# The last token block's norm, divided between GpSimd and VectorE, with its second half in one PSUM bank

## The chip, the cores and the metric

The kernel runs on one core of a Trainium2 chip. The metric is the time of one execution on the device in microseconds. A core has five engines with instruction streams of their own: TensorE (PE in the profile; its weight loads are PEld), VectorE (DVE), ScalarE (ACT), GpSimd (POOL) and SyncE (SP). They work on SBUF, TensorE writes its products into PSUM, which is divided into banks of 512 f32 columns by 128 partitions, and DMA queues move data between SBUF and HBM.

## The reference

Two transformer layers over 512 tokens of width 1024, in float32. Layer 0 mixes with latent attention, layer 1 with sliding-window attention; each layer then has an MLP of inner width 4096. After every part comes a layer norm of the scaled input plus the part's output:

```python
def _layernorm(x, g, b):
    xf = x.astype(jnp.float32)
    mu = xf.mean(-1, keepdims=True)
    var = jnp.square(xf - mu).mean(-1, keepdims=True)
    return ((xf - mu) * lax.rsqrt(var + LN_EPS) * g + b).astype(x.dtype)

def _mlp(x, w_up, w_down):
    h = jax.nn.relu(x @ w_up)
    return (h * h) @ w_down

def reference(...):
    ...
    for l in range(DEPTH):
        ...
        x = _layernorm(alpha * x + y, ln_mix_g[l], ln_mix_b[l])
        x = _layernorm(alpha * x + _mlp(x, mlp_w_up[l], mlp_w_down[l]), ln_mlp_g[l], ln_mlp_b[l])
    return x
```

The change concerns the very last of these norms, that of layer 1's MLP, whose result is the output.

## The kernel before

Products in float32 are made of three matmuls each: both factors are split into a high and a low part (`split`), and `three` lists high by high, high by low and low by high. The 512 tokens are four blocks of 128 (`NT` = 4). The last stage of each MLP is a `TokMajor` product: tokens lie on the partitions, the 1024 output columns are two halves of 512, and the sum over 1024 inner features runs over four weight chunks `kp` of two feature blocks each, so a block of tokens by half of the columns takes 24 matmuls.

`TokMajor.finish` first runs the first half of the columns, chunk by chunk over the four token blocks (`part`, which hands a block's bank to `evac` after its last chunk). It then fetches all four weight chunks of the second half, and goes through the token blocks one by one: 24 matmuls into a bank, `evac`, and the block's `layer_norm`. For the last norm (`dst is None`) of the last block, the second half is two accumulations of 256 columns, each into a bank of its own.

Here `evac` is `add_last`: VectorE adds the bank to the token rows `xs[t]` in SBUF (`add_plain`, L563) and `count` gathers the statistics (`bn_stats`, L553; in pieces of 256 columns for the last block, of 512 for the others). `layer_norm` aggregates them (L419), lets GpSimd raise the variance to the power -1/2 (`rsqrt_of`, L398), and makes two passes on VectorE: subtract the mean and multiply by the gain (L422), multiply by the rsqrt and add the bias (L425). The last block's second pass is cut at 512 and 768, and SyncE stores each cut (L428); the other blocks are stored whole.

PSUM tiles come from a ring of six full banks (`bank`), whatever their width; a bank comes free when the last user of its tile is done. The order of the instructions on an engine is set by a planner that reckons the time of each and issues what is ready by priority: earlier program order first, and what stands in `tc.high_priority()` ahead of the rest. Only what is passed to `pe` (all matmuls here) keeps the program's order; `pin` does so for VectorE in other stages, and not in this one. The planner also puts in the semaphores between engines that use the same tile.

Of the kernel before, what the change touches and what calls it, by code (L numbers as in the profile page):

```python
# [8 lines left out]
F32 = mybir.dt.float32  # L9
F32R = mybir.dt.float32r  # L10
AF = mybir.ActivationFunctionType
ALU = mybir.AluOpType
# [3 lines left out]
P = 128  # L16
D = 1024
S = 512
NT = S // P
# [29 lines left out]
def build(tc, nc, io, out):  # L49
    with ExitStack() as top:  # L50
# [3 lines left out]
        sp = top.enter_context(tc.tile_pool(name="sp", bufs=1))  # L54
# [7 lines left out]
        def nm(s):  # L62
            n_names[0] += 1
            return f"{s}_{n_names[0]}"

        def bank(cols=512, tag="mm", bufs=6):
            return ps.tile([P, cols], F32, tag=tag, bufs=bufs, name=nm(tag), padded_shape=[P, 512])
# [17 lines left out]
        def pe(ins):  # L85
            tc.keep_in_program_order(ins)

        pinned = [False]
# [8 lines left out]
        def pin(ins):  # L97

            if pinned[0]:
                pe(ins)  # L100

        def group(dst, pairs, first=True, last=True, **kw):
            for i, (st, mv) in enumerate(pairs):
                pe(nc.tensor.matmul(  # L104
                    dst, st, mv, start=first and i == 0, stop=last and i == len(pairs) - 1, **kw
                ))
# [186 lines left out]
        state = {"next": 0, "at": 0, "hold": 0}  # L293
# [6 lines left out]
        def prepare(n):  # L300

            state["hold"] += n
            while state["next"] < state["hold"]:
                prep(state["next"])
                state["next"] += 1

        def weights(name):
            i = state["at"]
            state["at"] += 1
            while state["next"] < len(stream):  # L310
                on_ring = len([j for j in range(i, state["next"] + 1) if not off_ring[j]])
                if on_ring > AHEAD or state["next"] >= state["hold"] or (off_ring[state["next"]] and mlp_pool[0] is None):
                    break
                prep(state["next"])
                state["next"] += 1
            got, wh, wl = ready.pop(i)
            assert got == name
            return wh, wl
# [7 lines left out]
        class Feat:  # L326


            def __init__(self):
                self.hs, self.ls = xt_pair()  # L330
# [13 lines left out]
        b = bank()  # L344
# [51 lines left out]
        def rsqrt_of(v):  # L396
            r = sp.tile([P, 1], F32, tag="rs", bufs=8, name=nm("rs"))
            nc.gpsimd.tensor_tensor(r, v, half, ALU.pow)  # L398
            return r


        xs = [None] * NT

        def load_gb(which, l):

            if which == "mix":
                gb = [mlp_pool[0].tile([P, D], F32, tag=tag, bufs=1, name=nm("gb")) for tag in ("a12", "a22")]
            else:
                both = gp.tile([P, 2, D], F32, tag="gb", bufs=1, name=nm("gb"))
                gb = [both[:, 0, :], both[:, 1, :]]  # L410
            for to, of in zip(gb, "gb"):
                pe(nc.sync.dma_start(to, io[f"ln_{which}_{of}"][l].partition_broadcast(P)))
            return gb

        def layer_norm(t, gb, dst):

            x = xs[t]
            mv = sp.tile([P, 2], F32, tag="mv", bufs=4, name=nm("mv"))
            pin(nc.vector.bn_aggr(mv, stats[t]))  # L419
            stats[t] = None  # L420
            r = rsqrt_of(mv[:, 1:2])
            pin(nc.vector.scalar_tensor_tensor(x, x, mv[:, 0:1], gb[0], ALU.subtract, ALU.mult))  # L422
            cuts = (0, 512, 768, D) if dst is None and t == NT - 1 else (0, D)
            for c in map(slice, cuts, cuts[1:]):
                state["norm"] = nc.vector.scalar_tensor_tensor(x[:, c], x[:, c], r, gb[1][:, c], ALU.mult, ALU.add)  # L425
                pin(state["norm"])
                if dst is None:
                    nc.sync.dma_start(out[t * P : (t + 1) * P, c], x[:, c])  # L428

        def turn_tokens(t, dst):  # L430

# [19 lines left out]
        class TokMajor:  # L451
# [4 lines left out]
            def __init__(self, src, evac, name):  # L456
                self.src, self.evac, self.name = src, evac, name
                self.w, self.b, self.done = [], {}, set()

            def group(self, b, t, kp, w, cols=slice(0, 512)):  # L460
                tk = slice(t * P, (t + 1) * P)
# [5 lines left out]
            def part(self, t, kp):  # L467
                while len(self.w) <= kp:
                    self.w.append(weights(self.name))
                if t not in self.b:  # L470
                    self.b[t] = bank()
                self.group(self.b[t], t, kp, self.w[kp])
                self.done.add((t, kp))
                if kp == 3:
                    self.evac(t, slice(0, 512), self.b[t])

            def finish(self, gb=None, dst=None, early=None):

                for kp in range(4):
                    for t in range(NT):
                        if (t, kp) not in self.done:
                            self.part(t, kp)
                if gb is not None:
                    ws = [weights(self.name) for _ in range(4)]
                    if callable(gb):
                        gb = gb()
                    for t in range(NT):
                        n = 2 if dst is None and t == NT - 1 else 1  # L490
                        for i in range(n):
                            c = slice(i * 512 // n, (i + 1) * 512 // n)
                            b = bank(512 // n)
                            for kp in range(4):
                                self.group(b, t, kp, ws[kp], c)
                            pinned[0] = early
                            with tc.high_priority():
                                self.evac(t, slice(512 + c.start, 512 + c.stop), b)
                            pinned[0] = False
                        pinned[0] = early  # L500
                        with tc.high_priority():
                            layer_norm(t, gb, dst)
                        if early:
                            prepare(early[t])
                        pinned[0] = False
                        if dst is not None and t in (1, 2):
                            with tc.high_priority():
                                dst.turn(t - 1)
                else:
                    bs = [bank() for _ in range(NT)]  # L510
                    for kp in range(4):
                        w = weights(self.name)
                        for t in range(NT):
                            self.group(bs[t], t, kp, w)
                    for t in range(NT):
                        self.evac(t, slice(512, D), bs[t])
# [27 lines left out]

        stats = [None] * NT

        def count(t, c):

            n = 256 if t == NT - 1 else 512
            if stats[t] is None:  # L550
                stats[t] = sp.tile([P, D // n, 6], F32, tag="bn", bufs=4, name=nm("bn"), padded_shape=[P, 4, 6])
            for i in range(c.start // n, c.stop // n):
                pin(nc.vector.bn_stats(stats[t][:, i, :], xs[t][:, i * n : (i + 1) * n]))  # L553
                if i == 0:

                    m2 = stats[t][:, 0, 2:3]
                    pin(nc.vector.tensor_scalar(m2, m2, LN_EPS * D, None, ALU.add))
# [7 lines left out]
        def add_scaled_last(t, c, b):  # L565
            add_scaled(t, c, b)
            count(t, c)

        def add_last(t, c, b):
            add_plain(t, c, b)  # L570
            count(t, c)
# [310 lines left out]
        with tc.tile_pool(name="mla", bufs=1) as mp:  # L882
# [108 lines left out]
            ws = [weights("w_q") for _ in range(4)]  # L991
# [98 lines left out]
            ws = [weights("w_qr"), weights("w_qr")]  # L1090
            qb = {}
            for t, rs in ((0, (0, 1)), (1, (0, 1)), (0, (2,)), (1, (2,)), (2, range(3)), (3, range(3))):
                tk = slice(t * P, (t + 1) * P)
                if 0 in rs:
                    qb[t] = bank()
                for r in rs:
                    wh, wl = ws[r // 2]
                    c = slice((r % 2) * 512, (r % 2 + 1) * 512)
# [110 lines left out]
        gb = lambda: load_gb("mix", 0)  # L1209
# [10 lines left out]
        with tc.tile_pool(name="swa", bufs=1) as mp:  # L1220
# [55 lines left out]
            def queries(m, part):  # L1276
                if part == 0:
                    qb[m] = (weights("w_sq"), bank())
                w, b = qb[m]
                feat_major(x2, w, b, ks=range(4 * part, 4 * part + 4))  # L1280
                if part == 1:
                    load_bias(m)
                    with tc.high_priority():
                        query_parts(m, slice(0, S), b)
# [118 lines left out]
        gb = lambda: load_gb("mix", 1)  # L1403
# [115 lines left out]
```

## Time and profile before

| what | value |
|---|---|
| median of 3 runs | 997.08 us (996.8 to 997.32) |
| span of the profiled execution | 997.4 us |
| TensorE busy in the span | 986.3 us (99%) |
| VectorE busy | 771.9 us (77%) |
| ScalarE busy | 554.7 us (56%) |
| GpSimd busy | 216.5 us (22%) |
| start of the last matmul | 989.76 us |
| start of the last store | 994.34 us |

The profiled execution has no time of its own beside its span; the three runs are timed apart from it. A row of a timeline is: start in us, length in us, engine, line, operation, output<-inputs, shapes, count, and in brackets the idle time before it with what ended it. A row of the groups is: line, engine, operation, tiles, shapes, count, then busy time in us and the mean in ns of one, then the idle time of the engine just before them. "SPq" and "ACTq" are the queues that issue DMAs. A row of the issues ends with the time in us from an issue to its landing. The ends of matmuls are modelled; their starts are measured.

### The profile page before, as it was taken

How to read it: one execution, taken by the hardware profiler on the slowest of the kernel's cores; microseconds unless marked ns; L12 is line 12 of the kernel's file. 1: busy time of each engine (PE TensorE's matmuls, PEld its weight loads, DVE VectorE, ACT ScalarE, POOL GpSimd, SP SyncE). 2: the span in 40 equal slices, each digit the busy share in tenths (PEclk: the TensorE clock that was granted, in tenths of full speed). 3: DMA queues.
4: the chain of work that ended last, by engine and by line, in shares of the span. 5: the costliest groups of instructions: out<-in, count | busy, mean ns of one | idle time of the engine just before them, and what ended most of it. 6: DMA issues, size and time to landing. Idle time of an engine off the chain costs nothing.

```text
span 997.4 us, 15835 instructions
## 1 busy us (share of the span) xinstructions
PE 986.3 (99%) x6107; PEld 890.0 (89%) x6107; DVE 771.9 (77%) x1243; ACT 554.7 (56%) x850; POOL 216.5 (22%) x203
## 2 busy tenths in 40 slices
PE   9999999999999999999999999999999999999997
PEld 8988888998999999998898998889998999999986
DVE  5589967989778769877586778698985986898756
ACT  5457643467537637636145888546763664664620
POOL 0231101122212211210002775212131122123000
PEclk9999999999999999999999999999999999999999
DMA  7431126389879977963232212259798798798422
GB/s 249 143 89 54 64 106 224 92 174 243 157 171 241 175 174 202 230 118 125 87 106 96 85 65 75 96 158 208 195 187 187 166 214 175 162 263 147 117 93 85
DMA packets 60679, 149.55 MB, mean 150 GB/s; under 512 B 5260, under 2 KB 10301, under 8 KB 60605
## 3 DMA queue, kind: packets, MB, share of 16 engines
q0 software_dynamic: 24320, 58.73, 32.9%
q1 hardware_dynamic: 36140, 89.56, 27.1%
q8 instruction: 48, 0.79, 0.3%
q10 hardware_dynamic: 144, 0.26, 0.1%
q14 instruction: 27, 0.21, 0.1%
HBM read 146.41 MB, written 4.22 MB: 151 GB/s over the span
## 4 chain that ended last, share of the span: by engine, by line
PE 96%; DVE 2%; ACT 1%; DMA 1%; issue 0%; POOL 0%; DVEq 0%; SPq 0%; ACTq 0%
PE mm L104 88%; PE tr L104 5%; PE tr L1159 1%; PE tr L663 1%; PE tr L1348 1%; ACT wh L77 1%; PE tr L1350 0%; DMA raw<-in_w_kv 0%; PE tr L437 0%; DMA raw<-in_w_h 0%; DVE mm L1320 0%; DVE ptl L80 0%; PE tr L924 0%; DVE ql L80 0%; POOL wl L80 0%
## 5 line engine op out<-in xcount | busy, mean ns | idle before, releaser
L104 PE MATMUL mm<-wh,fac 128*128 128x512 f32 (+1 forms) x944 | 292.8, 387 | 0.0
L77 ACT ACTIVATE wh<-wq 128x1024 fp32r<-128x1024 f32 x164 | 173.6, 1060 | 183.6 <-PE mm L104 131.4
L80 DVE TENSOR_TENSOR wl<-wq,wh 128x1024 fp32r<-128x1024 f32 x164 | 199.7, 1222 | 70.9 <-ACT wh L77 70.1
L104 PE MATMUL mm<-xth,wh 128*128 128x256 f32 (+1 forms) x928 | 243.7, 291 | 0.0
L104 PE MATMUL mm<-xth,wl 128*128 128x256 f32 (+1 forms) x800 | 233.5, 292 | 0.0
L104 PEld LDWEIGHTS mm<-wh,fac 128*128 128x128 f32 x944 | 176.3, 188 | 35.4 <-DVE fac L80 0.6
L104 PE MATMUL mm<-xtl,wh 128*128 128x256 f32 (+1 forms) x672 | 197.4, 294 | 0.0
L104 PE MATMUL mm<-wl,fac 128*128 128x512 f32 (+1 forms) x472 | 182.4, 387 | 0.0
L104 PEld LDWEIGHTS mm<-xth,wh 128*128 128x128 f32 x928 | 168.9, 192 | 3.1
L104 PEld LDWEIGHTS mm<-xth,wl 128*128 128x128 f32 x800 | 153.4, 192 | 2.6
L77 ACT ACTIVATE wh<-raw 128x1024 fp32r<-128x1024 f32 (+3 forms) x86 | 85.0, 989 | 95.1 <-PE mm L104 56.4
L199 POOL DMA_DIRECT2D wq<-in_up x64 | 77.5, 1228 | 257.7 <-DVE wl L80 189.0
L104 PEld LDWEIGHTS mm<-xtl,wh 128*128 128x128 f32 x672 | 128.9, 192 | 3.0
L80 DVE TENSOR_TENSOR wl<-raw,wh 128x1024 fp32r<-128x1024 f32 (+2 forms) x66 | 77.1, 1174 | 35.1 <-ACT wh L77 34.7
L104 PEld LDWEIGHTS mm<-wl,fac 128*128 128x128 f32 x472 | 88.9, 188 | 16.6
L199 POOL DMA_DIRECT2D wq<-in_down x48 | 42.0, 875 | 187.5 <-DVE wl L80 181.6
L80 POOL TENSOR_TENSOR wl<-raw,wh 128x1024 fp32r<-128x1024 f32 (+2 forms) x20 | 41.2, 2063 | 87.6 <-ACT wh L77 81.9
L104 PE MATMUL mm<-wh,oh 128*128 128x512 f32 x128 | 50.9, 398 | 0.0
L104 PE MATMUL mm<-wh,ol 128*128 128x512 f32 x128 | 50.2, 392 | 0.0
L104 PE MATMUL mm<-wl,oh 128*128 128x512 f32 x128 | 50.0, 390 | 0.0
L398 POOL TENSOR_TENSOR rs<-mv,half 128x1 f32<-128x1 f32 x16 | 11.0, 689 | 167.2 <-DVE mv L419 167.1
L563 DVE TENSOR_TENSOR x<-mm,x 128x512 f32<-128x512 f32 (+1 forms) x49 | 32.9, 676 | 14.5 <-PE mm L104 14.5
(217 smaller groups left out, 1822.3 us busy)
## 6 DMA issues: line engine op xcount, KB each, us to landing
wq<-in_up POOLq DMA_DIRECT2D x64, 512.0 KB, 8.5
wq<-in_down POOLq DMA_DIRECT2D x48, 512.0 KB, 7.1
wq<-in_up SPq DMA_DIRECT2D x32, 512.0 KB, 7.0
raw<-in_down SPq DMA_DIRECT2D x28, 512.0 KB, 6.8
wq<-in_down SPq DMA_DIRECT2D x24, 512.0 KB, 5.4
raw<-in_up SPq DMA_DIRECT2D x16, 512.0 KB, 4.6
raw<-in_w_o SPq DMA_DIRECT2D x8, 512.0 KB, 4.2
raw<-in_w_sq SPq DMA_DIRECT2D x8, 512.0 KB, 3.3
```

The lines of the kernel that those rows point to most:

```text
L77: high = nc.scalar.activation(dst_h, src, AF.Copy)
L80: low = (engine or nc.vector).tensor_sub(dst_l, src, f32(dst_h))
L104: pe(nc.tensor.matmul(dst, st, mv, start=first and i == 0, stop=last and i == len(pairs) - 1, **kw))
L199: nc.gpsimd.dma_start(half(a, jp), chunk(*more, jp), accum_op=ALU.add)
L398: nc.gpsimd.tensor_tensor(r, v, half, ALU.pow)
L563: nc.vector.tensor_add(xs[t][:, c], b, xs[t][:, c])
L663: pe(nc.tensor.transpose(pt[:, a, :], xs[t][:, k * P : (k + 1) * P], ident))
L1159: pe(nc.tensor.transpose(pt[:, kb * P : (kb + 1) * P], p[:, kb * P : (kb + 1) * P], ident))
L1348: pe(nc.tensor.transpose(pt[:, a, 0:P], p[:, kb, P:256], ident))
```

## The change

For the last norm of the last token block (`tail` is set and `t == NT - 1`):

- In the first half, the bank's columns 0 to 255 are added into SBUF as before, and columns 256 to 511 are added in place: VectorE adds the token rows to the bank and leaves the sum there (`add_in` without `to`). The bank is kept to the end.
- The second half is one bank with two accumulations of 256 columns. After each, VectorE adds the token rows in place and counts from the bank.
- `last_norm` takes the place of `layer_norm`. After the aggregate and the rsqrt, GpSimd takes columns 0 to 255 in SBUF in three instructions, and VectorE the other 768: a first pass of 256 and 512 columns within the banks, and a second pass of three times 256 columns from the banks into SBUF. SyncE stores columns 256 to 767 and then 768 to 1023, ScalarE's queue columns 0 to 255.
- Neither `add_in` nor `last_norm` stands in `tc.high_priority()`.

For the other token blocks and the other products the instructions stay as they were.

```diff
@@ layer_norm, last_norm @@
             pin(nc.vector.scalar_tensor_tensor(x, x, mv[:, 0:1], gb[0], ALU.subtract, ALU.mult))
-            cuts = (0, 512, 768, D) if dst is None and t == NT - 1 else (0, D)
-            for c in map(slice, cuts, cuts[1:]):
-                state["norm"] = nc.vector.scalar_tensor_tensor(x[:, c], x[:, c], r, gb[1][:, c], ALU.mult, ALU.add)
-                pin(state["norm"])
-                if dst is None:
-                    nc.sync.dma_start(out[t * P : (t + 1) * P, c], x[:, c])
+            state["norm"] = nc.vector.scalar_tensor_tensor(x, x, r, gb[1], ALU.mult, ALU.add)
+            pin(state["norm"])
+            if dst is None:
+                nc.sync.dma_start(out[t * P : (t + 1) * P, :], x)
+
+        def last_norm(t, gb, low, high):
+            x, tk = xs[t], slice(t * P, (t + 1) * P)
+            mv = sp.tile([P, 2], F32, tag="mv", bufs=4, name=nm("mv"))
+            nc.vector.bn_aggr(mv, stats[t])
+            r = rsqrt_of(mv[:, 1:2])
+            c = slice(0, 256)
+            nc.gpsimd.tensor_scalar(x[:, c], x[:, c], mv[:, 0:1], r, ALU.subtract, ALU.mult)
+            nc.gpsimd.tensor_mul(x[:, c], x[:, c], gb[0][:, c])
+            nc.gpsimd.tensor_add(x[:, c], x[:, c], gb[1][:, c])
+            for b, c in ((low[:, 256:], slice(256, 512)), (high, slice(512, D))):
+                nc.vector.scalar_tensor_tensor(b, b, mv[:, 0:1], gb[0][:, c], ALU.subtract, ALU.mult)
+            for b, c in ((high[:, :256], slice(512, 768)), (low[:, 256:], slice(256, 512)), (high[:, 256:], slice(768, D))):
+                nc.vector.scalar_tensor_tensor(x[:, c], b, r, gb[1][:, c], ALU.mult, ALU.add)
+                if c.start == 256:
+                    nc.sync.dma_start(out[tk, 256:768], x[:, 256:768])
+                elif c.start == 768:
+                    nc.sync.dma_start(out[tk, c], x[:, c])
+            nc.scalar.dma_start(out[tk, 0:256], x[:, 0:256])
@@ TokMajor.part @@
-                if kp == 3:
+                if kp == 3 and self.tail and t == NT - 1:
+                    add_in(t, slice(0, 256), self.b[t][:, 0:256], xs[t][:, 0:256])
+                    add_in(t, slice(256, 512), self.b[t][:, 256:512])
+                elif kp == 3:
                     self.evac(t, slice(0, 512), self.b[t])
@@ TokMajor.finish @@
+                self.tail = gb is not None and dst is None
...
                     for t in range(NT):
-                        n = 2 if dst is None and t == NT - 1 else 1
-                        for i in range(n):
-                            c = slice(i * 512 // n, (i + 1) * 512 // n)
-                            b = bank(512 // n)
-                            for kp in range(4):
-                                self.group(b, t, kp, ws[kp], c)
-                            pinned[0] = early
-                            with tc.high_priority():
-                                self.evac(t, slice(512 + c.start, 512 + c.stop), b)
-                            pinned[0] = False
+                        b = bank()
+                        if self.tail and t == NT - 1:
+                            for i in range(2):
+                                c = slice(i * 256, (i + 1) * 256)
+                                for kp in range(4):
+                                    self.group(b[:, c], t, kp, ws[kp], c)
+                                add_in(t, slice(512 + c.start, 512 + c.stop), b[:, c])
+                            last_norm(t, gb, self.b[t], b)
+                            break
+                        for kp in range(4):
+                            self.group(b, t, kp, ws[kp])
+                        pinned[0] = early
+                        with tc.high_priority():
+                            self.evac(t, slice(512, D), b)
@@ count @@
+        def add_in(t, c, b, to=None):
+            to = b if to is None else to
+            nc.vector.tensor_add(to, b, xs[t][:, c])
+            count(t, c, to)
+
+        def count(t, c, src=None):
...
-                pin(nc.vector.bn_stats(stats[t][:, i, :], xs[t][:, i * n : (i + 1) * n]))
+                pin(nc.vector.bn_stats(stats[t][:, i, :], xs[t][:, i * n : (i + 1) * n] if src is None else src))
```

More of the change, by code (lines that the diff above doesn't have):

```diff
@@ L458, in __init__ @@
                 self.w, self.b, self.done = [], {}, set()
+                self.tail = False
             def group(self, b, t, kp, w, cols=slice(0, 512)):
@@ L545, in build @@
         stats = [None] * NT
-        def count(t, c):
+        def add_in(t, c, b, to=None):
[3 more added lines that the diff above has]
+        def count(t, c, src=None):
             n = 256 if t == NT - 1 else 512
```

## The prediction

> **What bounds the kernel now.** I read the page first (busy shares, then the chain that ended last), then that chain in order of time over the last 12 us, then the timelines of VectorE, TensorE, SyncE and GpSimd there.
>
> ```profile
> PE 986.3 (99%) x6107; PEld 890.0 (89%) x6107; DVE 771.9 (77%) x1243; ACT 554.7 (56%) x850; POOL 216.5 (22%) x203
> PE 96%; DVE 2%; ACT 1%; DMA 1%; issue 0%; POOL 0%; DVEq 0%; SPq 0%; ACTq 0%
> ```
>
> TensorE is busy 99% of the span and carries 96% of the chain. So two things alone can move the end: a hole in TensorE's work, and what runs after its last matmul. The chain of waits shows the second part, here as start, length, engine and line:
>
> ```profile
> 990.08 0.44 DVE x L563
> ...
> 990.54 0.44 DVE bn L553
> ...
> 991.00 0.28 DVE mv L419
> ...
> 991.30 1.32 DVE x L422
> ...
> 992.71 0.75 DVE x L425
> 993.46 0.40 DVEq L1515
> 993.86 0.40 DVE x L425
> ```
>
> After the last matmul VectorE adds 256 columns, counts them (bn), aggregates (done at 991.26; I call this moment A), and makes two passes over the 1024 columns, the second in three cuts. SyncE stores each cut:
>
> ```profile
> 994.34 0.45 SPq L428 DMA_DIRECT2D out<-x  x1
> out<-x SPq DMA_DIRECT2D x2, 128.0 KB, 2.2
> ```
>
> The last store is issued at 994.34, A + 3.08, and lands 2.2 us later, at 996.5; 0.9 us of closing work follows up to 997.4. That store sets the end.
>
> **The change: the tail behind A.** Removed are one pass over 1024 columns and one over 512+256+256. In their place VectorE makes 256+512 and then 256+256+256, and GpSimd does three instructions on 256 columns behind its own rsqrt. The rows for both:
>
> ```profile
> L425 DVE SCALAR_TENSOR_TENSOR x<-x,rs,gb 128x256 f32<-128x256 f32 x2 | 0.9, 480 | 0.0
> L927 DVE SCALAR_TENSOR_TENSOR cq<-tr,gq,cq 128x512 fp32r<-128x512 f32 x3 | 2.1, 742 | 0.0
> L1320 DVE CUSTOM_DVE_ANT_0 mm<-mm,bias 128x256 f32<-128x256 f32 x48 | 20.5, 427 | 1.6
> 991.34 0.55 POOL L398 TENSOR_TENSOR rs<-mv,half 128x1 f32<-128x1 f32 x1 [4.72 <-DVE mv L419]
> L1335 POOL TENSOR_TENSOR p<-p,ri 128x128 f32<-128x128 f32 x16 | 6.4, 400 | 25.8 <-DVE ri L1334 14.1 <-ACT pth L77 10.6 <-PE mm L104 0.7
> L1337 POOL TENSOR_TENSOR p<-p,ri 128x768 f32<-128x768 f32 x16 | 23.5, 1467 | 0.0
> L80 POOL TENSOR_TENSOR wl<-raw,wh 128x512 fp32r<-128x512 f32 x1 | 1.3, 1299 | 0.0
> L80 POOL TENSOR_TENSOR wl<-raw,wh 128x1024 fp32r<-128x1024 f32 x12 | 28.7, 2398 | 54.4 <-ACT wh L77 51.3 <-PE mm L104 3.0
> 0.99 0.38 ACTq L352 DMA_DIRECT2D xraw<-in_xT  x1
> ```
>
> VectorE: a scalar_tensor_tensor of 256 columns takes 0.48, one of 512 from PSUM 0.74 (0.75 from SBUF in the chain, so PSUM costs nothing extra; L1320 even reads and writes PSUM, 256 columns in 0.43). Two that don't depend on each other overlap by 0.08 (starts 0.40 apart for 256: 993.86 less 993.46); one that reads the other's result starts 0.10 after its end (991.30 + 1.31, then 992.71). So behind A: 0.04 to 0.52, then 0.44 to 1.18, then three at 1.28, 1.68 and 2.08, the last ending at 2.56. SyncE's first store goes at about 2.2, its second 0.04 to 0.09 behind the end, at 2.62.
>
> GpSimd: rsqrt ends at 0.63. An instruction with two full operands costs 1299 ns at 512 and 2398 at 1024 columns, 2.15 ns a column and 0.2 fixed: 0.75 at 256, for the product with gb[0] and for the sum with gb[1]. The tensor_scalar with two per-partition numbers has no row. Above, it is bounded by the instructions with one broadcast operand (400 at 128, 1467 at 768: 0.61 at 256); below, by the 0.40 of 128 columns. I take 0.5, between them. End: 0.65 + 0.5 + 0.75 + 0.75 = 2.65, bounds 2.55 and 2.76. ScalarE, idle by then, issues the third store at 2.7 (its one earlier issue took 0.38, against 0.45 on SyncE); nothing is queued behind it there. So the last issue moves from A + 3.08 to A + 2.7: **0.4 us saved**, bounds 0.28 (GpSimd at its upper bound) and 0.45 (SyncE's second store last).
>
> **The change: one bank in place of two.** Before, the last token block's second half was two accumulations in two banks; now both lie in one, and VectorE's add and count of the first piece read and write that bank while TensorE is due to write the second piece into it. The rows around it:
>
> ```profile
> 986.88 0.40 PE L104 MATMUL mm<-wh,fac 128*128 128x256 f32 x2
> 986.03 1.31 DVE L422 SCALAR_TENSOR_TENSOR x<-x,mv,gb 128x1024 f32<-128x1024 f32 x1
> 986.07 0.55 POOL L398 TENSOR_TENSOR rs<-mv,half 128x1 f32<-128x1 f32 x1 [4.89 <-DVE mv L419]
> 987.26 0.41 DVE L563 TENSOR_TENSOR x<-mm,x 128x256 f32<-128x256 f32 x1
> 987.59 1.27 DVE L425 SCALAR_TENSOR_TENSOR x<-x,rs,gb 128x1024 f32<-128x1024 f32 x1
> 988.78 0.41 DVE L553 BATCH_NORM_STATS2 bn<-x 128x6 f32<-128x256 f32 x1
> 989.76 0.28 PE L104 MATMUL mm<-wh,fac 128*128 128x256 f32 x1
> L104 PE MATMUL mm<-wh,fac 128*128 128x256 f32 x32 | 5.9, 283 | 0.0
> L104 PE MATMUL mm<-wl,fac 128*128 128x256 f32 x16 | 4.5, 283 | 0.0
> ```
>
> 32 + 16 matmuls are two pieces of 24, started 0.12 apart. The second piece starts at 987.00 (the second matmul of the first row quoted), its last at 989.76. VectorE's add of the first piece runs from 987.26, its count from 988.78 to 989.19, since the second pass of token block 2's norm stands between them. Today TensorE passes both by, in another bank. The trace shows no case of TensorE writing a bank while VectorE works on it, so the cost is bounded: nothing below, if the two may overlap; above, until the count is done. I take the upper end: both pieces are one tile, VectorE now writes into it, and every other bank in this kernel is emptied only after all the matmuls into it. What TensorE loses when VectorE releases it:
>
> ```profile
> 610.83 0.58 DVE ptl L80
> 611.55 0.30 PE L1348 MATMUL tr<-ident,p 128*128 128x128 f32 x1 [0.89 <-DVE ptl L80]
> ```
>
> VectorE ends at 611.41, TensorE starts 0.14 later; the shortest such step the other way is 0.04 (last matmul 990.04, add 990.08). With 0.1, the second piece starts at 989.29 in place of 987.00: **2.29 us lost**, bounds 2.23 and 2.34 with VectorE's order as it is. The order is the other unknown. The add is no longer marked urgent, while the norm of block 2 still is. But the norm stood ahead of the add before, too, and was passed over, presumably because its rsqrt was not done yet in the planner's reckoning; so I keep add, norm, count. What is queued behind the held matmuls is only the rest of that piece, and VectorE's work on it.
>
> The Trainium skill (PSUM — Partial Sum Buffer, section "PSUM bank collisions raise a hardware error") says that TensorE and VectorE may not touch one bank at the same time, at other columns either, that the chip doesn't stall by itself, and that the program must put a semaphore between them bank by bank. By that rule the hold is full, 2.29; by the lower bound it is nothing. No row here tests it.
>
> **What costs nothing.** In the first half of block 3, one add of 512 becomes two of 256 with their counts. That is some 0.1 us more VectorE time near 968, and the next user is the split of a weight:
>
> ```profile
> 969.87 1.21 DVE L80 TENSOR_TENSOR wl<-raw,wh 128x1024 fp32r<-128x1024 f32 x1
> 973.45 0.69 DVE L563 TENSOR_TENSOR x<-mm,x 128x512 f32<-128x512 f32 x1 [2.24 <-PE mm L104]
> 974.83 0.39 PE L104 MATMUL mm<-wl,fac 128*128 128x512 f32 x1
> 975.51 0.39 PE L104 MATMUL mm<-wl,fac 128*128 128x512 f32 x1
> ```
>
> That split ends at 971.08. TensorE needs it for the last 6 matmuls before 973.41 (the add at 973.45 follows by 0.04). Matmuls of 512 columns start 0.227 apart (the two rows are three matmuls apart, 0.68), so the six start at about 972.0; 0.9 us of cover are left, and VectorE idles 2.24 us afterwards. Without the cover it would cost that 0.1. The low bank is held to the end, but of six banks the second half takes two free ones and those of blocks 0 and 1, emptied long before.
>
> **Sum.** 997.4 + 2.29 - 0.4 = 999.3 for the span. The runs' median lies 0.3 under the profiled span (997.08), so **999.0**, bounds from 998.85 (2.23 less 0.45, added to 997.08, rounded) to 999.15 (2.34 less 0.28).
>
> **The rivals.**
> - No hold: the pieces overlap in one bank, and only the tail counts. 997.08 - 0.4 = 996.7. For it: no row shows a hold. Against: VectorE writes into the tile whose other half TensorE writes. This is the side of "not slower".
> - A shorter hold: the count comes straight behind the add (both done at 988.13, by the steps 990.08, 990.54 and 0.43), so the second piece starts at 988.23 and loses 1.23: 997.9. Against: the planner put the norm between them before.
> - A longer hold, on the slower side: the norm's second pass goes first because the add has lost its mark. It would start at 987.44 (0.10 behind the first pass), the add at 988.64, the count at 989.10 to 989.51, the matmul at 989.61: 2.61 lost, 999.3. It decides as soon as the norm's rsqrt is reckoned ready at the end of the first pass (on the chip it was: 986.07 + 0.55 is before 987.34).
> - The clock drops in the hole. At the start of the kernel, before TensorE had worked, matmuls of 512 columns were 0.47 apart (below), against 0.227 later, so 24 matmuls would take 2.9 us more: 1001.9. Against: after the hole of 0.89 quoted above TensorE went on at its old pace. The Trainium skill (TensorE: Matmul & The Clock Gate, section "Part 1: The HAM clock gate (the "warmup" mystery)") lets the clock fall after an idle window of about 3.4 us; by that rule a hole of some 2 us would not do it.
> - GpSimd becomes the last: it decides once its three instructions take more than 2.4 us together. At the price of the 512-column row, 1.3 each, the last store is issued at A + 4.6, so the tail loses 1.5 in place of saving 0.4: 1000.9. Against: their operands are half as long.
>
> ```profile
> 1.00 4.21 PE L104 MATMUL mm<-zeros 128*128 128x512 f32 x9 [1.00 <-POOL zeros L343]
> ```
>
> **How the numbers follow.** Forecast 0.58; longer hold 0.10; shorter hold 0.10; no hold 0.12; GpSimd last 0.06; clock 0.04. What a measurement of this kernel tells from no change is about 0.2%, 2 us: the marks are 995.1 and 999.07. The forecast stands just under the upper one; I put a third of it above (0.19), with the longer hold (0.09 of 0.10), GpSimd (0.05) and the clock (0.04): slower 0.37. Faster by over 2 us needs a gain that no term here gives: 0.03. Within: 0.60. The likeliest case alone spans 998.8 to 999.4. The range reaches down to the case without a hold, whose best is 996.6, and up to 1000.0, the longer hold with GpSimd slow as well; the clock and the worst of GpSimd, 0.1, stay outside.
>
> **What would show it.** TensorE idle about 2.2 us ahead of the second piece of 256 columns, released by VectorE's count: the hold is right, and its length tells the order. The last matmul near 992.3. VectorE's last pass ending 2.5 to 2.6 us behind the aggregate, GpSimd's sum at about 2.65, ScalarE's store last. No hole in TensorE, matmuls over 0.2 apart behind it, or a GpSimd instruction over 0.8 would prove me wrong.

## The result, and the profile after

The change makes the kernel slower: a median of 1002.36 us (1001.3 to 1003.07, five runs) against 997.08 (996.8 to 998.94, five runs), a ratio of 1.0049 with a 95% interval of 1.0037 to 1.0060. That is 5.3 us where 1.9 were forecast, and outside the range (996.6 to 1000.0).

The chain of waits of the changed kernel, in order of time (start, length, what), has the answer in three places:

```profile
985.75 0.06 DVE mm L575
985.81 0.20 issue
986.01 1.27 DVE x L423
987.28 0.35 DVE bn L584
987.63 0.04 issue
987.68 4.31 PE mm L104 x24
...
992.95 0.27 DVE mv L431
993.22 0.07 issue
993.29 0.55 POOL rs L398
...
993.94 1.22 POOL x L434
...
995.25 0.72 POOL x L435
995.97 0.04 issue
996.01 0.76 POOLq L1546
```

First, the hold stands as forecast: add, norm, count, and only then TensorE. Second, the 24 matmuls behind it take 4.31 us, where 23 steps of 0.12 and the last one's 0.28 make some 3.0. Third, the chain then runs through GpSimd to the end, with 1.22 for the tensor_scalar. The timeline of TensorE around the hold, and the windows over the same stretch (length; busy time and count of PE, PEld, DVE, ACT and POOL; granted clock, DMA share, GB/s):

```profile
985.30 0.28 PE L104 MATMUL mm<-wh,fac 128*128 128x256 f32 x1
987.68 0.39 PE L104 MATMUL mm<-wh,fac 128*128 128x256 f32 x1 [2.10 <-DVE bn L584]
```

```profile
985.40:987.60 2.20, 0.18 (x2) 0.00 (x0) 2.20 (x4) 0.00 (x0) 0.00 (x0) 1.00 0.00 0
987.60:989.00 1.40, 1.32 (x11) 1.33 (x12) 0.02 (x1) 0.00 (x0) 0.00 (x0) 1.00 0.64 257
989.00:990.00 1.00, 1.00 (x8) 1.00 (x7) 0.00 (x0) 0.00 (x0) 0.00 (x0) 0.60 0.41 164
990.00:991.00 1.00, 1.00 (x7) 1.00 (x6) 0.00 (x0) 0.00 (x0) 0.00 (x0) 0.50 0.00 0
991.00:992.00 1.00, 0.97 (x5) 0.68 (x4) 0.00 (x0) 0.00 (x0) 0.00 (x0) 0.50 0.00 0
```

TensorE is idle for 2.10 us until VectorE's count is done. It then works for 1.5 us at full clock, and from about 989.2 on at half (0.60 is the mean of 989.00 to 990.00). In this execution the clock falls after the hole, while TensorE is busy again; e6 below shows that it need not be so late. The timeline of all engines behind the aggregate:

```profile
993.29 0.55 POOL L398 TENSOR_TENSOR rs<-mv,half 128x1 f32<-128x1 f32 x1 [8.25 <-DVE mv L431]
993.94 1.22 POOL L434 TENSOR_SCALAR x<-x,mv,rs 128x256 f32<-128x256 f32 x1
994.30 1.26 DVE L440 SCALAR_TENSOR_TENSOR x<-mm,rs,gb 128x256 f32<-128x256 f32 x3
...
995.25 0.72 POOL L435 TENSOR_TENSOR x<-x,gb 128x256 f32<-128x256 f32 x1
995.59 0.42 SPq L444 DMA_DIRECT2D out<-x  x1
996.05 0.72 POOL L436 TENSOR_TENSOR x<-x,gb 128x256 f32<-128x256 f32 x1
996.80 0.35 ACTq L445 DMA_DIRECT2D out<-x  x1
```

VectorE and SyncE are done by 996.0; GpSimd ends at 996.77. The last store is issued at 996.80, which is A + 3.59 (the aggregate ends at 993.21), and the span ends 3.4 us later, at 1000.2.

### The profile page after: what moved, and what is told of

Same layout as the page of the kernel before. It is cut to its first block, busy times and chain, and to the rows that moved or that the text cites. A ratio compares the mean times of both kernels' runs of the same rounds, so it can differ in the third digit from the quotient of the medians.

```text
span 1000.2 us, 15843 instructions
## 1 busy us (share of the span) xinstructions
PE 986.1 (99%) x6107; PEld 889.3 (89%) x6107; DVE 771.3 (77%) x1245; ACT 555.0 (55%) x850; POOL 219.2 (22%) x206
## 4 chain that ended last, share of the span: by engine, by line
PE 95%; DVE 2%; ACT 1%; DMA 1%; POOL 0%; issue 0%; POOLq 0%; SPq 0%; DVEq 0%; ACTq 0%
PE mm L104 87%; PE tr L104 5%; PE tr L1190 1%; PE tr L694 1%; PE tr L1379 1%; ACT wh L77 1%; PE tr L1381 0%; DMA raw<-in_w_kv 0%; DMA raw<-in_w_h 0%; PE tr L454 0%; DVE mm L1351 0%; PE tr L955 0%; DVE ptl L80 0%; DVE ql L80 0%; POOL wl L80 0%
## 5 line engine op out<-in xcount | busy, mean ns | idle before, releaser
L594 DVE TENSOR_TENSOR x<-mm,x 128x512 f32<-128x512 f32 x46 | 31.4, 686 | 14.5 <-PE mm L104 14.4
```

The source lines that it names most:

```text
L594: nc.vector.tensor_add(xs[t][:, c], b, xs[t][:, c])
```

## How the runs are compared

Up to the first add of the last block's second half all kernels do almost the same work, but single executions reach that point up to 2.7 us apart (984.56 in e2, 987.26 in the first profile of before). So the stages behind that add are compared, each read from the timelines of one profiled execution. "Outside" is the execution's own time less its span. The row of before is that of experiment c0, whose execution has both.

| kernel | first add to second add | second add to A | A to last store issued | to the end of the span | outside | sum | median, with that of before beside it |
|---|---|---|---|---|---|---|---|
| before (c0) | 2.81 | 1.19 | 3.08 | 3.04 | 1.74 | 11.86 | 997.41 / 997.53 |
| the change | 6.33 | 1.20 | 3.59 | 3.40 | 2.16 | 16.68 | 1002.36 / 997.08 |
| e1, two banks | 2.82 | 1.19 | 3.61 | 3.41 | 2.16 | 13.19 | 998.52 / 997.53 |
| e3, TensorE kept busy | 5.18 | 1.19 | 3.60 | 3.41 | 2.17 | 15.55 | 1000.58 / 997.53 |
| e2, no GpSimd | 6.40 | 1.19 | 3.20 | 3.05 | 1.89 | 15.73 | 1000.29 / 997.53 |
| e4, count first | 4.10 | 1.20 | 3.59 | 3.46 | 2.10 | 14.45 | 1000.07 / 997.32 |
| e5, store on SyncE | 6.58 | 1.19 | 3.59 | 3.45 | 2.13 | 16.94 | 1002.94 / 997.32 |
| e6, trials on GpSimd | 6.67 | 1.20 | 3.60 | 3.44 | 2.12 | 17.03 | 1002.52 (one run) / 997.32 |
| e8, one bank only | 3.64 | 1.18 | 3.08 | 2.97 | 1.84 | 12.71 | 997.93 / 997.32 |
| e9, idle work on GpSimd | 2.82 | 1.19 | 3.59 | 3.99 | 1.80 | 13.39 | 998.57 / 997.54 |
| e7, 128 on GpSimd | 2.82 | 1.18 | 3.19 | 3.42 | 1.82 | 12.43 | 997.75 / 997.54 |

Of the 4.8 us between the first two rows, 3.5 lie ahead of A and 1.3 behind it. The remaining 0.5 to the medians' 5.3 is within the scatter of single executions.

## The experiments

**c0: the kernel before once more**, for a span and a time of the same execution. No edit.

> The kernel before, unchanged, to see its spans beside its times. 997.1. If its span lies 2.2 us under the time, as the changed kernel's does, then the profiled execution of before (span 997.4) was a slow one, and the whole change costs 5.3 us of span; if span and time agree, 2 us of the difference arise outside the span.

997.41, and a span of 995.6 in an execution of 997.34: 1.74 lie outside the span. So the profiled execution of before (span 997.4) was itself one of some 999.1, 2 us over the median. Both answers of the expectation are part of the truth: most of the difference is in the span, and 0.4 (2.16 less 1.74) outside it. That part is steady: every execution of c0 has 1.72 to 1.85 outside, every one of the change 2.12 to 2.20.

**e1: each piece in a bank of its own.** The hold is taken away by giving the second piece another bank.

```diff
...
-                        b = bank()
                         if self.tail and t == NT - 1:
+                            bs = []
                             for i in range(2):
                                 c = slice(i * 256, (i + 1) * 256)
+                                bs.append(bank(256))
                                 for kp in range(4):
-                                    self.group(b[:, c], t, kp, ws[kp], c)
-                                add_in(t, slice(512 + c.start, 512 + c.stop), b[:, c])
-                            last_norm(t, gb, self.b[t], b)
+                                    self.group(bs[i], t, kp, ws[kp], c)
+                                add_in(t, slice(512 + c.start, 512 + c.stop), bs[i])
+                            last_norm(t, gb, self.b[t], bs)
                             break
+                        b = bank()
```

(VectorE's first pass then has three instructions of 256 columns instead of 256 and 512.)

> The change, but each piece of the second half of the last token block again has a bank of its own. Theory H (the shared bank holds TensorE, and its clock falls in the hole: 2.3 us and some 1.4 us): the second piece follows the first at once, 0.12 us from matmul to matmul, and the time is 1002.4 - 3.7 = 998.7. Rival T (the tail on GpSimd is what costs): no more than 0.5 us less than the change, 1001.9 or above.

998.52, ratio to before 1.0011 (1.0002 to 1.0020). The stretch between the adds is that of before, 2.82. Theory H holds: 3.5 of the 4.8 us are the shared bank's. What stays, 1.3 by the table and 1.0 by the medians, is the tail's, and it is a loss, not the saving of 0.4 that was forecast.

**e3: TensorE kept busy during the hold.** Nine matmuls of zeros into a spare bank.

```diff
                                 add_in(t, slice(512 + c.start, 512 + c.stop), b[:, c])
+                                if i == 0:
+                                    idle = bank().rearrange("p (a b) -> p a b", a=4)
+                                    group(idle, [(zeros, zeros[:, None, :].broadcast_to([P, 4, P]))] * 9)
```

> The change, with nine matmuls of zeros (2.0 us) into a spare bank between the two pieces, so that TensorE isn't idle while it is held. Theory H with the clock: the granted clock stays at 1.0, the second piece takes 2.9 us instead of 4.3, and the time is 1002.4 - 1.4 = 1001.0, though the hold itself stays. Rival (the second piece is slow because of the bank it shares, not because TensorE was idle): it stays at 4.3 us, and the time at 1002.4.

The timeline has the nine matmuls, the chain of waits the second piece, and the windows its clock:

```profile
984.87 2.23 PE L104 MATMUL mm<-zeros 128*128 128x512 f32 x9
```

```profile
987.12 3.15 PE mm L104 x24
```

```profile
987.10:988.50 1.40, 1.38 (x11) 1.38 (x12) 0.00 (x0) 0.00 (x0) 0.00 (x0) 1.00 0.68 275
988.50:989.50 1.00, 1.00 (x10) 1.00 (x9) 0.00 (x0) 0.00 (x0) 0.00 (x0) 1.00 0.35 139
989.50:990.30 0.80, 0.76 (x7) 0.55 (x5) 0.00 (x1) 0.00 (x0) 0.00 (x0) 1.00 0.00 0
```

The nine matmuls end at 987.10, where VectorE's count ends too (987.07). Same hold, same bank, same 24 matmuls, 3.15 us instead of 4.31, and the clock stays at 1.00. Median 1000.58. So it is TensorE's idleness in the hold that lowers the clock, and the two parts of the hold separate: 2.4 us (5.18 less 2.81) for the waiting, 1.2 (6.33 less 5.18) for the clock.

**e4: a shorter hold.** Block 2's norm is written behind the first piece's add, and its second pass is issued after the count.

```diff
...
+                                if i == 0:
+                                    layer_norm(NT - 2, gb, dst, (state["count"],))
...
+            with behind(after):
+                state["norm"] = nc.vector.scalar_tensor_tensor(x, x, r, gb[1], ALU.mult, ALU.add)
...
```

> The change, but VectorE counts the first piece straight behind its add, and the second pass of block 2's norm comes after, so TensorE is held some 1.0 us instead of 2.1. Theory H with a clock that falls only after a long enough hole (0.9 us elsewhere did not lower it): the granted clock stays at 1.0, the second piece takes 3.1 us, and from the first add to the second pass 4.0 us instead of 6.3; time 1002.4 - 2.2 = 1000.2. Rival (any hole of 1 us lowers it here): the piece stays at 4.3, first add to second 5.2, time 1001.3.

The chain of waits around the hold, in order of time:

```profile
986.00 0.44 DVE bn L589
986.45 0.04 issue
986.49 3.14 PE mm L104 x24
```

1000.07, as theory H said: TensorE is idle for 1.04 us, and the clock does not fall (the windows show 1.00 throughout). Between the adds the shorter hold is worth 2.2 us, 1.08 of waiting (5.18 less 4.10) and 1.15 of the clock (6.33 less 5.18).

**e8: the hold without the rest.** The kernel before, with the two pieces in one bank; sums and counts stay in SBUF, so TensorE waits only for the add.

```diff
+                        whole = bank()
                         for i in range(n):
                             c = slice(i * 512 // n, (i + 1) * 512 // n)
-                            b = bank(512 // n)
+                            b = whole[:, c]
```

> The kernel before, with the last block's second half in one bank, in two pieces as in the change; the sums still go to SBUF and are counted there, and the norm is as before. The hold by itself: TensorE waits only for the add, which is done 0.4 us after its start, so the second piece starts 0.8 us later than before, at full clock: from the first add to the second 3.6 us instead of 2.8; time 997.5 + 0.8 = 998.3. Rival (the planner holds the bank until the count, as in the change): 6.3 us, time 1001.

The timeline of TensorE where the second piece begins, and the piece in the chain of waits:

```profile
985.40 0.39 PE L104 MATMUL mm<-wh,fac 128*128 128x256 f32 x1 [0.56 <-DVE x L564]
985.62 0.28 PE L104 MATMUL mm<-wl,fac 128*128 128x256 f32 x1
```

```profile
985.40 3.14 PE mm L104 x24
```

997.93, ratio 1.0008 (0.9999 to 1.0016). The add releases TensorE after 0.56 us, the 24 matmuls take 3.14 as in e4, and the adds are 3.64 apart, 0.83 more than before. So by this stage one bank alone costs 0.8 (the medians, 0.6 apart, are not clear of noise); it is the count from PSUM, queued behind block 2's norm, that makes 3.5 of it, the clock's 1.2 included.

**e2: GpSimd's share undone.** VectorE takes columns 0 to 255 in SBUF.

```diff
-            nc.gpsimd.tensor_scalar(x[:, c], x[:, c], mv[:, 0:1], r, ALU.subtract, ALU.mult)
-            nc.gpsimd.tensor_mul(x[:, c], x[:, c], gb[0][:, c])
-            nc.gpsimd.tensor_add(x[:, c], x[:, c], gb[1][:, c])
+            nc.vector.scalar_tensor_tensor(x[:, c], x[:, c], mv[:, 0:1], gb[0][:, c], ALU.subtract, ALU.mult)
...
+            nc.vector.scalar_tensor_tensor(x[:, c], x[:, c], r, gb[1][:, c], ALU.mult, ALU.add)
```

> The change, but VectorE also takes columns 0 to 255 (two instructions in SBUF); GpSimd has the rsqrt alone. Theory H: the last store is issued some 3.4 us after the aggregate instead of 3.6, so the time is within 0.4 us of the change (1002.0 to 1002.4). Rival T: it falls by 1 us or more, to 1001.4 or below.

1000.29, ratio to before 1.0032 (1.0020 to 1.0045) against the change's 1.0049 (1.0037 to 1.0060). Here theory H missed: by the medians the time fell by 2.1 us, as the rival said, though the two intervals overlap and e2's five runs spread from 999.74 to 1002.2. The stages show 1.0 of it: 0.4 since the last store is issued at A + 3.20, as expected, and 0.6 more behind that store (3.05 and 1.89 instead of 3.40 and 2.16), which nobody had in the sum. The other 1.1 lies ahead of the first add (984.56 in e2's profile, 985.68 in the change's), where both do the same work: it is scatter. The hold is still there (6.40), so the rival is not the main cause either: both are true, and the end of the program was missing in each.

**e5: the last store on SyncE's queue.**

```diff
-            nc.scalar.dma_start(out[tk, 0:256], x[:, 0:256])
+            nc.sync.dma_start(out[tk, 0:256], x[:, 0:256])
```

> The change, with the last store on SyncE's queue instead of ScalarE's. Theory Q (a store on ScalarE's queue that comes last lengthens the end: 3.40 us from its issue to the end of the span and 2.16 outside it, against 3.05 and 1.74 with SyncE last): 3.05 to 3.1 and about 1.75 to 1.9, so 0.6 us less than the change, 1001.7. Rival (the longer end belongs to GpSimd's late finish): unchanged, 1002.3.

1002.94, with 3.45 and 2.13 behind the last store. Theory Q falls: with SyncE's queue last, the end is as long as with ScalarE's. The rival, GpSimd's late finish, stays. The instructions of the closing line show what it may be: GpSimd's closing instruction, DRAIN, in the changed kernel and, in the second row, in the kernel before (c0; count, length in ns, start):

```profile
L1546 POOLq DRAIN  x1: 3429/3429/3429, 996.0 to 996.0; - x1
```

```profile
L1515 POOLq DRAIN  x1: 3256/3256/3256, 989.5 to 989.5; - x1
```

It starts with GpSimd's last instruction and is over some 2.7 us after that one's end. Before, that is at 992.8, long before SyncE has seen its stores land (about 994.7). In the changed kernel it is at 999.4, and SyncE is through at 998.8: GpSimd is the last.

**e9: the same GpSimd work, on a tile that nobody uses**, in the kernel before. It computes nothing for the output.

```diff
...
+            if dst is None and t == NT - 1:
+                nc.gpsimd.tensor_scalar(trial, trial, mv[:, 0:1], r, ALU.subtract, ALU.mult)
+                nc.gpsimd.tensor_mul(trial, trial, gb[0][:, 0:256])
+                nc.gpsimd.tensor_add(trial, trial, gb[1][:, 0:256])
```

> The kernel before, with the change's three GpSimd instructions added behind the last rsqrt, on a tile that nothing else uses; banks, stores and VectorE's work are those of before. Theory G (the program cannot close until GpSimd's closing drain is over, some 2.7 us after its last instruction): the last store is still issued 3.1 us after the aggregate, but the span ends 3.4 us behind GpSimd's last instruction, 7.0 us after the aggregate instead of 6.1, and with some 0.3 us more outside the span the time is 997.4 + 1.2 = 998.6. Rival (only the stores set the end): 997.4, span end 6.1 us after the aggregate.

The timeline of all engines behind the last rsqrt:

```profile
989.85 1.71 POOL L426 TENSOR_SCALAR trial<-trial,mv,rs 128x256 f32<-128x256 f32 x1
990.56 2.12 DVE L432 SCALAR_TENSOR_TENSOR x<-x,rs,gb 128x512 f32<-128x512 f32 x3
991.45 1.60 SPq L435 DMA_DIRECT2D out<-x  x3
991.64 0.76 POOL L427 TENSOR_TENSOR trial<-trial,gb 128x256 f32<-128x256 f32 x1
992.48 0.78 POOL L428 TENSOR_TENSOR trial<-trial,gb 128x256 f32<-128x256 f32 x1
```

The third of the stores in the row of SyncE starts at 992.71.

998.57, ratio 1.0009 (1.0000 to 1.0018). The span ends at 996.7, 3.44 after GpSimd's last instruction (993.26), in keeping with theory G: 3.99 behind the last store instead of 3.04, though no store waits for that work. Two points were off: the store itself came at A + 3.59 (below, contention), and outside the span there were only 1.80, so the 2.1 to 2.2 outside the span in the change, e1, e3, e4, e5 and e6 are not explained by GpSimd's late end.

**e6: what a tensor_scalar costs on GpSimd.** Six of them on an unused tile near the start.

```diff
...
+        for cols, op in ((256, ALU.mult), (128, ALU.mult), (256, None)):
+            for _ in range(2):
+                two = (half, op) if op else (None,)
+                nc.gpsimd.tensor_scalar(trial[:, :cols], trial[:, :cols], half, two[0], ALU.subtract, *two[1:])
```

> The change, with six tensor_scalar instructions on an otherwise unused tile on GpSimd near the start: twice 256 columns with two operations, twice 128 with two, twice 256 with one. Theory C (the first use costs): the first takes 1.2 us or more, the second 0.5 to 0.6, and the one in the norm falls to 0.6 as well. Rival P (the price is by the column and the operation): both of 256 take 1.2, of 128 about 0.7, with one operation 0.6 to 0.8, and the one in the norm stays at 1.22.

The groups of GpSimd in the first 5 us (behind the bar the busy time in us and the mean in ns):

```profile
L406 POOL TENSOR_SCALAR trial<-trial,half 128x256 f32<-128x256 f32 x2 | 2.4, 1216 | 0.2
L406 POOL TENSOR_SCALAR trial<-trial,half 128x128 f32<-128x128 f32 x1 | 0.8, 793 | 0.1
```

1002.52 in one run. The first and the second use of 256 columns cost the same (1.21 and 1.22), and the one in the norm stayed at 1.22: theory C falls. 256 columns with two operations cost 1.2 and 128 cost 0.8 (0.92 the second time, with VectorE at work), as the rival has it. Its price for one operation did not come out (1.44 and 1.55), but these two ran while VectorE worked in SBUF, so they tell nothing.

The end of this profile also shows something about the clock. The hold is the change's (2.10 us idle, the second piece from 987.49 on), but here the clock is at half from the first matmul on, and back at full before the piece ends. The windows of e6:

```profile
985.40:987.50 2.10, 0.01 (x1) 0.01 (x1) 2.04 (x4) 0.00 (x0) 0.00 (x0) 1.00 0.00 0
987.50:990.90 3.40, 3.40 (x16) 3.40 (x17) 0.00 (x0) 0.00 (x0) 0.00 (x0) 0.50 0.38 154
990.90:992.10 1.20, 1.20 (x10) 1.02 (x9) 0.00 (x0) 0.00 (x0) 0.00 (x0) 0.99 0.00 0
```

In the change and in e2 the 3.4 us at half begin some 1.5 us after the matmuls do; the first row is of the change, the second of e2:

```profile
989.20:992.60 3.40, 2.77 (x14) 2.48 (x12) 0.55 (x2) 0.00 (x0) 0.00 (x0) 0.50 0.06 23
```

```profile
988.00:991.40 3.40, 2.92 (x15) 2.62 (x13) 0.43 (x1) 0.00 (x0) 0.00 (x0) 0.50 0.08 33
```

**e7: a smaller share.** The kernel before, with GpSimd on 128 columns and VectorE on 896.

```diff
...
+            if last:
+                c = slice(0, 128)
+                nc.gpsimd.tensor_scalar(x[:, c], x[:, c], mv[:, 0:1], r, ALU.subtract, ALU.mult)
...
-            cuts = (0, 512, 768, D) if dst is None and t == NT - 1 else (0, D)
+            cuts = (128, 640, D) if last else (0, D)
...
```

> The kernel before, two banks and sums in SBUF, but GpSimd takes the first 128 columns of the last norm (three instructions) and ScalarE's queue stores them; VectorE takes 896 in one first pass and two second ones. With theory G: GpSimd ends about 2.6 us after the aggregate, so the end comes 3.4 us behind that, 6.0 after the aggregate, against 6.1 before: no difference that can be measured, 997.4. Rival (only the stores count): the last store is issued at 2.65 instead of 3.08, so 997.0, or 0.4 us faster in the span. A third: VectorE and GpSimd now both read SBUF with two operands, and if that slows either by half, the span ends later than 6.3 behind the aggregate.

997.75, ratio 1.0005 (0.9996 to 1.0014): no difference that can be measured. GpSimd's tensor_scalar of 128 columns took 1.15 and VectorE's piece of 384 took 0.85, in each other's company, so GpSimd ended at A + 3.16 and the span 3.45 later, 6.6 after A, beyond the 6.3 of the expectation's third case. No run gave a version that beats the kernel before.

## Why the prediction was wrong

- **The hold: right**, both in the planner's order (add, norm, count) and in its cost: the second piece started at 987.68 where 985.42 was its turn (985.30 + 0.12), 2.26 against 2.29 forecast.
- **"After the hole of 0.89 ... TensorE went on at its old pace": the step that failed first.** This row was taken as evidence for a hole of 2.1 us, and the clock given 4%. Holes of 0.56, 0.89 and 1.04 us were indeed followed by a clock of 1.00, but the hole of 2.10 was followed by 0.50 in all four profiles that have it. In the change that cost 1.2 us. It is less than the rival's 2.9, since only the last 12 or so of the 24 matmuls ran at half. The prediction also weighed a rule: the Trainium skill (TensorE: Matmul & The Clock Gate, section "Part 1: The HAM clock gate (the "warmup" mystery)") lets the clock fall after an idle window of about 3.4 us. The measured hole was shorter and the clock fell all the same, so the measurement decides.
- **"The tensor_scalar ... I take 0.5": mis-sized.** It takes 1.22, beyond the 0.8 that the prediction itself named as a sign of being wrong. Its "upper bound" came from another operation with a broadcast operand, which bounds nothing here. The two products were right (0.72 against 0.75); three gaps of 0.08 to 0.1 between GpSimd's dependent instructions were left out. GpSimd's end is A + 3.56 instead of 2.65, the last store A + 3.59 instead of 2.70: 0.5 lost where 0.4 was to be saved. The rival "GpSimd becomes the last" was right in kind, and its point of 2.4 us was passed (2.66 plus the gaps).
- **"That store sets the end": wrong for the change.** Behind GpSimd's last instruction come 2.7 us of drain, so the end of the span is its business: 0.36 more than with the stores alone. Another 0.4 outside the span (1.74 to 2.16) is seen and not explained: it is all but gone when GpSimd's three instructions are (e2, 1.81 to 1.90 in its five executions), yet the same three instructions in the kernel before do not bring it (e9, 1.73 to 1.83).
- **VectorE's tail: near.** Its last pass ended at A + 2.35 (994.30 + 1.26 less 993.21), 2.56 forecast. The second pass began at A + 1.09, before the first had ended (993.24 + 1.15, A + 1.18), and not 0.10 behind it. VectorE was not the last, so this changed nothing.
- **The offset of 0.3 between span and median** mixed two things: the time lies 1.74 above the span in c0, and the profiled execution of before was one of some 999.1. As only a difference was added to the median, this cost nothing.

In sum: forecast were 1.9, 2.3 for the hold less 0.4 for the tail. To these come 1.2 for the clock, 0.9 for GpSimd's chain, and twice 0.4 for the end: 4.8, the difference of the table's first two rows.

## What to carry to other kernels

On the engine that bounds the kernel, an idle stretch can cost more than its length (here 2.10 us of it cost another 1.2 by the clock): keep pieces that are evacuated separately in separate banks, or see that what releases the bank is not queued behind other work. Before work is handed to a slower engine at the very end, price each operation from a row of the same operation, and count that engine's own closing as well as its last result. A bound taken from a different operation is a guess.

## What the runs showed of the hardware

- **TensorE's clock.** After 2.10 us of idleness the granted clock went to 0.5 and stayed there for 3.4 us, in each of the four profiles with the full hold and nothing in it. The moment of the fall varies: 0.02 us after work had begun again in e6, 1.2 in e5, 1.5 in e2 and the change. So does the price: the piece took 4.31 (the change), 4.37 (e2), 4.55 (e5) and 4.65 us (e6), against 3.15 in e3. In the 3.4 us just before the fall TensorE had been idle for 1.9 to 2.1 us; with 1.04 us idle (e4) there was no fall. Whether the fall always comes is open: the fastest run of the change (1001.3), the fastest of e5 (1001.06) and one of e2 (1000.11) have a mean clock of 0.998, as all runs of e3 have, and the others 0.995 to 0.997; these three have no timeline.
- **GpSimd.** A tensor_scalar with two per-partition numbers costs 1.22 us at 256 columns and 0.8 at 128, more than a tensor_tensor (0.72 at 256). Its closing drain lasts 2.7 us beyond its last instruction.
- **Contention in SBUF.** In e9, VectorE's second pass takes 0.71 instead of 0.48 for 256 columns in SBUF while GpSimd works, and GpSimd's tensor_scalar 1.71 instead of 1.22. The row of VectorE's groups there (count, busy us, mean ns):

```profile
L432 DVE SCALAR_TENSOR_TENSOR x<-x,rs,gb 128x256 f32<-128x256 f32 x2 | 1.3, 710 | 0.0
```

In the change VectorE reads its first operand from PSUM, and three passes of 256 take 1.26 together (1.25 in e2, where GpSimd is idle), and GpSimd's tensor_scalar 1.22, as in e6 with VectorE idle. The Trainium skill (SBUF — State Buffer, section "Who interferes with whom") says that a VectorE instruction with two inputs in SBUF contends with GpSimd's reads and one with a single such input does not. The runs agree, e9 with the times above and the change with these. They do not show who waits for whom: in e9 VectorE's first pass, with two inputs in SBUF too, kept its 1.31 while GpSimd's tensor_scalar ran beside it. So keeping the sums in the banks did spare VectorE and GpSimd this contention; it was paid for elsewhere.
